# Variance of two tiles on quarters of the array, key transposes in halves, and the last key tile among the value products

## The chip, the cores and the metric

The kernel runs on one core of one Trainium2 chip. The engines of a core each work through a queue of their own, in order: PE (TensorE, the matrix products; its weight loads are listed apart as PEld), DVE (VectorE), ACT (ScalarE), POOL (GpSimd) and SP (SyncE, which issues the transfers). The metric is the time of one execution in microseconds, lower is better, median of three runs.

## The reference

A decoder trunk of two layers on 16 learned and 256 given tokens, T = 272 in all, D = 2048: an RWKV-7 mixer, a squared-ReLU MLP, a gated linear attention (GLA), another MLP. The change touches the RWKV-7 mixer alone:

```python
r = xr @ w_rkv[0]; k = xk @ w_rkv[1]; v = xv @ w_rkv[2]
w_log = -softplus(-(w0 + tanh(xw @ w1) @ w2)) - 0.5
a = sigmoid(a0 + (xa @ a1) @ a2)
g = sigmoid(xg @ g1) @ g2
kk = k * k_k per head; kk = kk / max(sqrt(sum(kk * kk)), 1e-12)
k = k * (1 + (a - 1) * k_a);  decay = exp(-exp(w_log))
# per token and head: S <- S diag(decay) + (S (-kk)) (kk a)^T + v k^T;  y = S r
mu = mean(y); var = mean(square(y - mu))            # per head of 64
y = (y - mu) * rsqrt(var + eps) * ln_w + ln_b
bonus = sum(r * k * r_k) * v
out = ((y + bonus) * g) @ w_o
```

There are 32 heads of 64, so a tile of 128 rows holds two heads, and the 2048 features are 16 such tiles.

## The kernel before

Everything is kept transposed, features on the 128 partitions and tokens along the free axis. A weight comes as `raw` tiles of 128x1024 float32. ACT rounds one to `hi` (L140), DVE subtracts to get `lo` (L141), and PE makes three products for each 128x128 piece (`mm3`, L163 to L165): `hi` by the high part of the activations, `hi` by their low part, `lo` by the high part. So every weight tile needs ACT, then DVE, then 24 products of PE. There are three buffers for `raw` and two each for `hi` and `lo`.

The RWKV mixer has these stages, one after the other. The receptance products come first, with the low-rank (LoRA) products for decay and learning rate between them (`lora`, sigmoids at L478 and L479, kept in `hres` for the first eight tiles and in `ca` for the others). Then the **key stage**, a loop over the 16 tiles `f` of keys. `keyproj` makes the products of tile `f` from two weights. `front` scales them (`kk`, L619) and squares them (`sq`, L620). `rest(f - 1)` stands between the two weights of the next tile and does all that follows for a tile: `sums` (L604, four quarter products of 64x64 for the squared norm of `kk` in bank `pm` and for the bonus of the tile before in bank `pu`), three exponentials, a logarithm (L633 to L638), some fifteen small operations on DVE (L300 is the helper of all element-wise ones, L641 makes `kn` for the bonus), and transfers of the results to memory (`ard`, `bkd`). From tile 9 on `scores` also makes the masked score matrices (`AM`, products L537), and from tile 12 on `inv`, the inversion of a triangular system, runs as 30 steps of two DVE operations (`upd`, `sysA`).

After the last tile come the **value products** `v_proj`, also sixteen tiles with two weights each. They are cut into units of one `mm3` each, and `R(n)` runs n units; the code puts the work of the recurrence between them. For a group g of eight heads' pairs and a chunk c of 64 tokens this is: `centre` (values transposed and centred into bank `pm`, copied out by ACT at L745), `keys` (keys transposed by L752 into a `pt` bank and a `pm` bank, copied out at L754), `inner`, `state`, `solve`, `learn`, `emit`. `merge`, `scores` and `inv` are in between again. `norm(g)` is a generator, run tile by tile for the four tiles of g: per tile the square, one full-array float32 product with a block matrix of ones (the variance, L841, bank `pry`), two products with the gate weights `g2` (L844), a logarithm and an exponential on ACT, and three operations on DVE. `split(g)` then makes the output products' operands of `hres`.

The order on PE is written out by hand (`manual_schedule`) in these parts, while the end of one such block and the start of the next may interleave. On ACT, DVE and SP a scheduler decides at build time by program order, by estimated times and by priority: the weight loads have a priority of 2000, small transfers of 4000, all else none. The before calls the first value products like this:

```python
        for i in ((0, 128), (128, 320)):
            fetch(1, ARs, ard, i)
        ahead()
        with tc.manual_schedule(engines={mybir.EngineType.PE}):
            R(43)
```

`fetch(1, ARs, ...)` loads the block of `AR` for the next score matrices from memory, into a pool (`win`) that takes the place of the key stage's pool `early`.

## Time and profile before

| | |
|---|---|
| median of three runs | 2384.78 us (2384.59 to 2385.85) |
| the profiled execution | 2384.69 us, span 2382.6 us |
| mean granted clock of PE | 0.998 |
| receptance and low-rank products end, key stage begins | about 160 us |
| value products begin | about 267 us |
| output products of the RWKV mixer begin to stand alone | about 546 us |
| DVE busy over the span | 1608.1 us |
| ACT busy over the span | 1251.8 us |

The span is the profiled execution from its first to its last instruction; times in a timeline count from its start. In the list of waits a row names an engine, the line that waited, what released it, and then the total, the count and the longest wait. In a timeline a row has start, duration, engine, line, operation, output and inputs with their shape, and how many instructions of a kind were joined into the row (`x4`); brackets hold the idle time before it and what ended it. A float32 product leaves two records. In a table by stretches each engine's busy time stands with the number of its instructions, then the granted clock of PE as a share of full speed, the share of the transfer engines and their rate.

### The profile page before, as it was taken

To read this page: it belongs to the slowest core of one execution; us is meant where nothing else is said; L and a number is where in the kernel's file an instruction comes from. 1 tells how busy PE (TensorE), PEld (TensorE's weight loads), DVE (VectorE), ACT (ScalarE), POOL (GpSimd) and SP (SyncE) were. 2 spreads that over 40 slices of the span, in tenths; PEclk is the share of its full clock that TensorE was granted. 3 is DMA by queue.
4 is the path that set the end of the run, shared out by engine and by line. 5 is a ranking of instruction groups with operands and counts; after the bars stand their busy time and mean duration, and the time that the engine had idled before them with its cause. 6 is when DMAs were issued, how large, how long until landed. Compare 5 with 4: busy or idle time off the path is not lost. (4 is left out here: it accounts for less than half of the span.)

```text
span 2382.6 us, 48158 instructions
## 1 busy us (share of the span) xinstructions
PE 2349.0 (99%) x19753; PEld 2231.2 (94%) x19753; DVE 1608.1 (67%) x2702; ACT 1251.8 (53%) x1995; POOL 12.4 (1%) x37
## 2 busy tenths in 40 slices
PE   9999899999999999999999999999999999999998
PEld 8888898889999999999999999999999999999997
DVE  8868976848555555555556777767666666666666
ACT  6478554556555344345344556645555445445444
POOL 0000000000000000000000000000000000000000
PEclk9999999999999999999999999999999999999999
DMA  5468654535555555555555555445555555555554
GB/s 209 160 205 301 225 172 142 150 93 173 186 189 192 188 192 188 190 191 188 193 187 192 193 172 176 163 172 197 180 201 203 201 199 202 203 199 200 203 201 170
DMA packets 157003, 449.18 MB, mean 189 GB/s; under 512 B 33968, under 2 KB 49968, under 8 KB 156784
## 3 DMA queue, kind: packets, MB, share of 16 engines
q1 hardware_dynamic: 156784, 446.11, 54.7%
q8 instruction: 155, 2.54, 0.4%
q14 instruction: 64, 0.52, 0.1%
HBM read 429.93 MB, written 14.42 MB: 186 GB/s over the span
## 5 line engine op out<-in xcount | busy, mean ns | idle before, releaser
L141 DVE TENSOR_TENSOR lo<-raw,hi 128x1024 fp32r<-128x1024 f32 (+1 forms) x818 | 927.0, 1140 | 529.9 <-ACT hi L140 521.5
L140 ACT CAST hi<-raw 128x1024 fp32r<-128x1024 f32 (+1 forms) x818 | 794.2, 978 | 926.9 <-PE pj L164 535.8
L163 PE MATMUL pj<-x,hi 128*128 128x272 f32 (+1 forms) x2624 | 747.6, 285 | 4.3 <-DVE r L300 1.8
L165 PE MATMUL pj<-x,lo 128*128 128x272 f32 (+1 forms) x2624 | 732.3, 279 | 2.2 <-DVE lo L141 2.2
L164 PE MATMUL pj<-x,hi 128*128 128x272 f32 (+1 forms) x2624 | 732.8, 279 | 0.2 <-DVE x L240 0.2
L163 PEld LDWEIGHTS pj<-x,hi 128*128 128x128 f32 x2624 | 497.6, 190 | 17.1 <-issue 8.4
L165 PEld LDWEIGHTS pj<-x,lo 128*128 128x128 f32 x2624 | 497.8, 190 | 3.7 <-DVE lo L141 3.4
L164 PEld LDWEIGHTS pj<-x,hi 128*128 128x128 f32 x2624 | 497.9, 190 | 3.4 <-issue 1.8
L196 PE MATMUL pj<-x,hi 128*128 128x512 f32 x1280 | 419.8, 382 | 0.1
L197 PE MATMUL pj<-x,lo 128*128 128x256 f32 x1280 | 348.7, 273 | 0.0
L196 PE MATMUL pj<-h,hi 128*128 128x512 f32 x1008 | 330.3, 382 | 0.0
L163 PE MATMUL pj<-h,hi 128*128 128x272 f32 (+1 forms) x1040 | 290.1, 279 | 0.0
L164 PE MATMUL pj<-h,hi 128*128 128x272 f32 (+1 forms) x1040 | 290.1, 279 | 0.0
L165 PE MATMUL pj<-h,lo 128*128 128x272 f32 (+1 forms) x1040 | 290.1, 279 | 0.0
L197 PE MATMUL pj<-h,lo 128*128 128x256 f32 x1008 | 274.8, 273 | 0.0
L196 PEld LDWEIGHTS pj<-x,hi 128*128 128x128 f32 x1280 | 241.9, 189 | 34.1 <-DVE x L1063 0.4
L197 PEld LDWEIGHTS pj<-x,lo 128*128 128x128 f32 x1280 | 245.8, 192 | 0.1
L196 PEld LDWEIGHTS pj<-h,hi 128*128 128x128 f32 x1008 | 190.5, 189 | 26.5
L163 PEld LDWEIGHTS pj<-h,hi 128*128 128x128 f32 x1040 | 196.6, 189 | 0.0
L164 PEld LDWEIGHTS pj<-h,hi 128*128 128x128 f32 x1040 | 196.6, 189 | 0.0
L165 PEld LDWEIGHTS pj<-h,lo 128*128 128x128 f32 x1040 | 196.6, 189 | 0.0
L197 PEld LDWEIGHTS pj<-h,lo 128*128 128x128 f32 x1008 | 193.5, 192 | 0.0
(276 smaller groups left out, 2071.3 us busy)
## 6 DMA issues: line engine op xcount, KB each, us to landing
raw<-mlp_w_d SPq DMA_DIRECT2D x512, 512.0 KB, 3.3
raw<-gla_in_d SPq DMA_DIRECT2D x98, 512.0 KB, 3.2
raw<-w_rkv_d SPq DMA_DIRECT2D x80, 512.0 KB, 3.9
raw<-gla_o_d SPq DMA_DIRECT2D x32, 512.0 KB, 3.2
raw<-w_r_d SPq DMA_DIRECT2D x16, 512.0 KB, 3.2
raw<-rw_oQ_d SPq DMA_DIRECT2D x16, 512.0 KB, 3.5
raw<-lora_d SPq DMA_DIRECT2D x8, 512.0 KB, 3.4
raw<-rw_oA_d SPq DMA_DIRECT2D x8, 512.0 KB, 3.4
```

The costliest lines, as they stand in the source:

```text
L140: nc.scalar.copy(hi[:, h], raw[:, h])
L141: nc.vector.tensor_tensor(out=lo[:, h], in0=raw[:, h], in1=hi[:, h].bitcast(F32), op=ALU.subtract)
L163: nc.tensor.matmul(out, hi[:, ws], xh, start=first, stop=False)
L164: nc.tensor.matmul(out, hi[:, ws], xl, start=False, stop=False)
L165: nc.tensor.matmul(out, lo[:, ws], xh, start=False, stop=last)
L196: nc.tensor.matmul(wide, hi[:, ws], xt, start=kt == 0, stop=False)
L197: nc.tensor.matmul(one, lo[:, ws], xt[:, 0], start=False, stop=kt == nk - 1)
```

## The change

Four edits, all in `rwkv`.

1. `norm(g)` makes the four squares of its group first (four buffers), and takes two tiles together: each variance is two products with quarters of the array, four in a row, the first tile's in bank `pry`, the second's in bank `pm` with its halves exchanged. The second tile's logarithm is then two activations of half the partitions.
2. The gate weights `g2` are fetched two tiles ahead.
3. `keys` transposes 64-row halves, sixteen products in place of eight, by turns into the `pt` and the `pm` bank, both of which it takes at the start.
4. The key stage's loop ends at tile 15; `rest(15)` runs after the fourth value unit, `sums(None)` (the last tile's bonus sums) after the sixteenth, and the pool `win` and the fetches of `AR` follow behind. `rest` runs at a priority of 600.

```diff
@@ -651,15 +651,14 @@
             nc.gpsimd.tensor_copy(WC[:, f], W[:, C : 4 * C1 : C1])
 
         with tc.manual_schedule(engines={ENG.PE}):
-            for f in range(KT + 1):
-                if f < KT:
-                    ps = (self.pry if f % 3 == 2 else self.pj)()[:, :T]
-                    keyproj(f, ps, 0)
+            for f in range(KT):
+                ps = (self.pry if f % 3 == 2 else self.pj)()[:, :T]
+                keyproj(f, ps, 0)
                 if f:
-                    rest(f - 1)
-                if f < KT:
-                    keyproj(f, ps, 1)
-                    front(f, ps)
+                    with tc.high_priority(offset=600):
+                        rest(f - 1)
+                keyproj(f, ps, 1)
+                front(f, ps)
                 if f == 1:
                     xv = [self.t(self.xp, [P, 2, T], "x", KT, F32R) for _ in range(KT)]
                     for kt in range(KT):
@@ -683,15 +682,7 @@
                 if f > 12:
                     for _ in range(6):
                         next(inv, None)
-            sums(None)
-        early.close()
-
-        win = ExitStack()
-        kp = win.enter_context(tc.tile_pool(name="win", bufs=1, side="right", reuse_waits="tile"))
-        ARs.append(self.t(kp, [P, 8, 320], "AR1"))
-        AMs.append(self.t(kp, [P, 2, 16, 128], "AM1"))
-        AMrs.append(self.t(kp, [64, 16, 64], "AMr"))
-        sb = self.t(kp, [P, 8, HEAD], "S")
+
         bank = lambda x: x.rearrange("p (h v) -> p h v", h=8)
         uvs, ras, bkts, rys, pSs = {}, {}, {}, {}, {}
 
@@ -731,6 +722,8 @@
             yield
 
 
+        heads = lambda x: x.rearrange("p (h v) -> p h v", h=8)
+
         def centre(g, c):
             full, n, nr = geom(c)[:3]
             pv = self.pm()
@@ -745,13 +738,14 @@
                 nc.scalar.copy(x[:nr, 8 * e : 8 * e + 8], pv[64 * e : 64 * e + nr].rearrange("p (h v) -> p h v", h=8))
 
         def keys(g, c):
-            bkts[g, c] = self.t(kp, [P, 8, P], "bkt", 1)
-            for e in range(2):
-                pb = self.pm() if e else self.ptr()
-                for p in range(4):
-                    nc.tensor.transpose(pb[:, p * P : (p + 1) * P], BKs[c > 1][:, 4 * e + p, c % 2 * 128 : c % 2 * 128 + 128],
-                                        self.ident)
-                nc.scalar.copy(bkts[g, c][:, 4 * e : 4 * e + 4], pb.rearrange("p (h v) -> p h v", h=4))
+            x = bkts[g, c] = self.t(kp, [P, 8, P], "bkt", 1)
+            pbs = [self.ptr(), self.pm()]
+            for f in range(8):
+                for q in range(2):
+                    nc.tensor.transpose(pbs[q][:, f * HEAD : (f + 1) * HEAD],
+                                        BKs[c > 1][half(q), f, c % 2 * 128 : c % 2 * 128 + 128], self.ident[half(q), half(q)])
+            for q in range(2):
+                nc.scalar.copy(x[:, :, half(q)], heads(pbs[q]))
 
 
         def inner(g, c):
@@ -825,27 +819,44 @@
             nc.scalar.copy(hres[:, 8 * g : 8 * g + 8, c * C : c * C + nr], ry[:, :, :nr])
 
         def norm(g):
+            fs = range(4 * g, 4 * g + 4)
+            sqs, g2s = {}, {}
 
             def square(f):
-                sq = self.t(kp, [P, T], "ysq", 2)
-                nc.scalar.activation(sq, hres[:, f], AF.Square)
-                return sq
-
-            nxt = square(4 * g)
+                if f in fs:
+                    sqs[f] = self.t(kp, [P, T], "ysq", 4)
+                    nc.scalar.activation(sqs[f], hres[:, f], AF.Square)
+
+            def load(f):
+                if f in fs:
+                    g2s[f] = self.t(kp, [P, 2, P], "g2", 2)
+                    nc.sync.dma_start(g2s[f], ap["g2"][f])
+
+            def spread(sq, va, x, y):
+                nc.scalar.activation(sq[x], va[y], AF.Ln, scale=1.0 / HEAD, bias=self.eps[GN_EPS][x])
+
+            for i in range(2):
+                load(fs[i])
+            for i in range(4):
+                square(fs[i])
             yield
-            for f in range(4 * g, 4 * g + 4):
-                sq = nxt
-                g2 = self.t(kp, [P, 2, P], "g2", 2)
-                nc.sync.dma_start(g2, ap["g2"][f])
-                va = self.pry()[:, :T]
-                nc.tensor.matmul(va, self.bones, sq, start=True, stop=True)
+            for f in fs:
+                if f % 2 == 0:
+                    vas = [self.pry()[:, :T], self.pm()[:, :T]]
+                    for i in range(2):
+                        for q in range(2):
+                            nc.tensor.matmul(vas[i][half(q ^ i)], self.bones[half(q), half(q)], sqs[f + i][half(q)],
+                                             start=True, stop=True)
                 pg = (self.ptr() if g else self.pu())[:, :T]
                 for i in range(2):
-                    nc.tensor.matmul(pg, g2[:, i], gs[i], start=i == 0, stop=i == 1)
-                nc.scalar.activation(sq, va, AF.Ln, scale=1.0 / HEAD, bias=self.eps[GN_EPS])
+                    nc.tensor.matmul(pg, g2s[f][:, i], gs[i], start=i == 0, stop=i == 1)
+                load(f + 2)
+                if f % 2 == 0:
+                    spread(sqs[f], vas[0], slice(0, P), slice(0, P))
+                    for q in range(2):
+                        spread(sqs[f + 1], vas[1], half(q), half(1 - q))
+                sq = sqs[f]
                 nc.scalar.activation(sq, sq, AF.Exp, scale=-0.5)
-                if f < 4 * g + 3:
-                    nxt = square(f + 1)
                 nc.vector.scalar_tensor_tensor(out=sq, in0=hres[:, f], scalar=self.vec("ln_w", f), in1=sq, op0=ALU.mult,
                                                op1=ALU.mult)
                 tt(rr[f], rr[f], sq, ALU.add)
@@ -959,11 +970,25 @@
         nothing = iter(())
         units1 = ((2, 0), (2, 1), (3, 0), (3, 1), (4, 0))
         self.split_parts = 2
+        ahead()
+        with tc.manual_schedule(engines={ENG.PE}):
+            R(4)
+            with tc.high_priority(offset=600):
+                rest(KT - 1)
+            R(12)
+            sums(None)
+        early.close()
+
+        win = ExitStack()
+        kp = win.enter_context(tc.tile_pool(name="win", bufs=1, side="right", reuse_waits="tile"))
+        ARs.append(self.t(kp, [P, 8, 320], "AR1"))
+        AMs.append(self.t(kp, [P, 2, 16, 128], "AM1"))
+        AMrs.append(self.t(kp, [64, 16, 64], "AMr"))
+        sb = self.t(kp, [P, 8, HEAD], "S")
         for i in ((0, 128), (128, 320)):
             fetch(1, ARs, ard, i)
-        ahead()
-        with tc.manual_schedule(engines={mybir.EngineType.PE}):
-            R(43)
+        with tc.manual_schedule(engines={ENG.PE}):
+            until(43)
             for c, e in units1:
                 some(inv, 5)
                 R(13)
```

`half(q)` is rows 64q to 64q + 63, `ENG` is `mybir.EngineType`, `until(43)` runs what is left of the first 43 units.

How this moves instructions is shown at three places. The first is ACT at the end of the low-rank products and the beginning of the key stage, from the last sigmoids (L478, L479) to the first `kk` and `sq` of the key stage; `iW` at L636 is an exponential of `rest`. Before:

```order
L478 ACTIVATE iW_1782<-pm_1778,vecs_126 128x272
L479 ACTIVATE ca_1777<-pry_1779,vecs_126 128x272
L496 ACT_TABLE_LOAD
L140 CAST hi_1870<-raw_1868 128x1024
L636 ACTIVATE iW_1898<-hres_72 128x272
L636 ACTIVATE iW_2047<-hres_72 128x272
L140 CAST hi_1926<-raw_1924 128x1024
L619 ACTIVATE kk_1863<-pj_1802,vecs_126 128x272
L620 ACTIVATE sq_1864<-kk_1863 128x272
```

The two exponentials stand behind both sigmoids and the one table load. In the change, the same stretch of ACT:

```order
L478 ACTIVATE iW_1782<-pm_1778,vecs_126 128x272
L636 ACT_TABLE_LOAD
L636 ACTIVATE iW_1898<-hres_72 128x272
L140 CAST hi_1870<-raw_1868 128x1024
L636 ACTIVATE iW_2047<-hres_72 128x272
L479 ACT_TABLE_LOAD
L479 ACTIVATE ca_1777<-pry_1779,vecs_126 128x272
L140 CAST hi_1926<-raw_1924 128x1024
L496 ACT_TABLE_LOAD
L619 ACTIVATE kk_1863<-pj_1802,vecs_126 128x272
L620 ACTIVATE sq_1864<-kk_1863 128x272
```

They stand ahead of the last sigmoid, and three table loads are there in place of one. Some 65 rows earlier the exponentials `W` (L633) of the first two tiles move ahead of sigmoids in the same way, with four table loads before and now; on PE the small products `pm`, `pry` of those sigmoids come later.

The second place is DVE in the value products, where tile 15's operations stand (`kn` from bank `pj`, then `bk`, `ar`, and the `kn` of L641 that the last sums take). Before, around the `lo` of the fifth value weight (`lo_3659`):

```order
L300 TENSOR_TENSOR kn_3474<-pj_3360,kn_3474 128x272
L300 TENSOR_TENSOR upd_3503<-sysA_2014 64x234
L300 TENSOR_TENSOR bk_1789<-kn_3474,iW_3473 128x4x64
L141 TENSOR_TENSOR lo_3659<-raw_3656,hi_3658 128x512 x2
L300 TENSOR_TENSOR bk_1789<-kn_3474,iW_3473 128x16
L300 TENSOR_TENSOR ar_1791<-r_30_104,W_1797 128x4x64
L300 TENSOR_TENSOR ar_1791<-r_30_104,W_1797 128x16
L641 SCALAR_TENSOR_TENSOR kn_3474<-r_30_104,vecs_126,kn_3474 128x272
```

In the change, behind the `lo` of the second value weight (`lo_3497`):

```order
L141 TENSOR_TENSOR lo_3497<-raw_3494,hi_3496 128x512 x2
L300 TENSOR_TENSOR bk_1788<-kk_3338,iW_3391 128x16
L300 TENSOR_TENSOR kn_3506<-pj_3360,kn_3506 128x272
L300 TENSOR_TENSOR upd_3348<-sysA_2014 64x184
L300 TENSOR_TENSOR bk_1789<-kn_3506,iW_3505 128x4x64
L300 TENSOR_TENSOR bk_1789<-kn_3506,iW_3505 128x16
L300 TENSOR_TENSOR ar_1791<-r_30_104,W_1797 128x4x64
L300 TENSOR_TENSOR ar_1791<-r_30_104,W_1797 128x16
L641 SCALAR_TENSOR_TENSOR kn_3506<-r_30_104,vecs_126,kn_3506 128x272
```

The tile's operations now stand ahead of the later steps of the inversion (`upd` of 64x184 in place of 64x234), so ten steps more come behind them. Ahead of the `lo` of the eleventh value weight DVE has 547 instructions before and 545 in the change. On SP the two fetches of `AR` stand behind three value weights' loads fewer.

The third place is PE at `norm(1)`, where the values of the second group have just been centred (`pm`, L739 before, L732 in the change). Before:

```order
L739 MATMUL pm_5969<-cst_125,hres_72 64x128 x8
L841 MATMUL pry_5983<-ysq_5873,cst_125 128x272
L844 MATMUL pt_5985<-gs_2_76,g_903_5981 128x272
L844 MATMUL pt_5985<-gs_3_77,g_903_5981 128x272
L163 MATMUL pj_6007<-x_5995,hi_5946 128x272
```

In the change:

```order
L732 MATMUL pm_6020<-cst_125,hres_72 64x128 x8
L848 MATMUL pry_6032<-ysq_5918,cst_125 64x272 x2
L848 MATMUL pm_6033<-ysq_5920,cst_125 64x272 x2
L852 MATMUL pt_6038<-gs_2_76,g_893_5914 128x272
L852 MATMUL pt_6038<-gs_3_77,g_893_5914 128x272
L163 MATMUL pj_6062<-x_6050,hi_5997 128x272
```

The variance of the group's second tile has moved up to the first one's place, into the bank that `centre` has just filled.

## The prediction

> **What bounds the kernel now.** I read the head of the page first.
>
> ```profile
> span 2382.6 us, 48158 instructions
> PE 2349.0 (99%) x19753; PEld 2231.2 (94%) x19753; DVE 1608.1 (67%) x2702; ACT 1251.8 (53%) x1995; POOL 12.4 (1%) x37
> ```
>
> TensorE (PE) has work for all but 33.6 us of the span, so time can only be had where PE stands still or where its work itself shrinks. Everything that the change touches lies in the RWKV stage. Next I read the waits of PE (total, times, longest), of which these lie in that stage:
>
> ```profile
> PE pu L604 <- DVE kn L641: 2.5, 1, 2.5
> PE pm L604 <- ACT sq L620: 1.9, 3, 0.9
> PE pj L163 <- DVE r L300: 1.8, 1, 1.8
> PE pt L537 <- DMA AR<-ard: 1.7, 1, 1.7
> PE pj L163 <- ACT hres L884: 1.4, 1, 1.4
> ```
>
> The timeline puts the three single waits for `kn`, AR and `hres` into the first value products, within 25 us:
>
> ```profile
> 274.71 0.38 PE L163 MATMUL pj<-x,hi 128*128 128x272 f32 x1 [1.40 <-ACT hres L884]
> 283.04 0.68 PE L604 MATMUL pu<-kn,cst 64*64 64x272 f32 x4 [2.50 <-DVE kn L641]
> 295.64 0.83 PE L537 MATMUL pt<-AR,BK 64*128 64x128 f32 x10 [1.72 <-DMA AR<-ard]
> ```
>
> The last query is the work of VectorE (DVE) by stretches (start and end, length, DVE busy and its count, PE's granted clock):
>
> ```profile
> 160.00:264.00 104.00, 91.64 (x219) 1.00 0.83 277
> 264.90:305.10 40.20, 37.96 (x102) 0.96 0.65 208
> 306.00:393.00 87.00, 52.95 (x117) 1.00 0.53 157
> 393.60:434.50 40.90, 39.12 (x103) 1.00 0.48 141
> 442.60:481.80 39.20, 37.11 (x101) 1.00 0.40 121
> 482.00:546.00 64.00, 32.36 (x65) 1.00 0.34 109
> ```
>
> This decides most of what follows. In the second, fourth and fifth stretch, in each of which a triangular inversion of 60 small operations runs, DVE is busy for 94 to 96% of the time: there PE follows DVE, and what PE saves comes back as a longer wait. From 306 to 393 and after 482 DVE has room, and a saving on PE shows in the end.
>
> **The last key tile among the value products.** A unit is three products with one 128-row piece of a weight. Before, the last sums (the wait of 2.5 us) stand behind 32 value units, in the change behind 16, and the tile's DVE work comes earlier to match. Its wait has a second price, the granted clock right behind it (here in the eleventh column of the windows of all engines):
>
> ```profile
> 284.60:287.80 3.20, 3.20 (x17) 3.20 (x16) 3.00 (x10) 0.33 (x1) 0.00 (x0) 0.50 0.44 124
> ```
>
> PE runs there at half clock for 3.2 us, which costs 1.6. Were PE alone to decide, the change would take out 1.4 + 2.5 + 1.7 (the transfer of AR, issued three weights earlier in SP's queue) + 1.6 = 7.2 us. That is the upper end. The lower one comes from DVE, and from PE behind it:
>
> ```profile
> 288.98 0.69 DVE L141 TENSOR_TENSOR lo<-raw,hi 128x512 fp32r<-128x512 f32 x1 [1.37 <-ACT hi L140]
> 305.10 0.68 DVE L141 TENSOR_TENSOR lo<-raw,hi 128x512 fp32r<-128x512 f32 x1
> 306.46 0.28 PE L163 MATMUL pj<-x,hi 128*128 128x272 f32 x1
> ```
>
> The row at 305.10 is the `lo` half of the eleventh value weight, which PE begins at about 306.4. DVE has 547 instructions ahead of that row before and 545 in the change, so nearly the same work must be done first, and what can be won is DVE's idle time, 40.20 - 37.96 = 2.2 us (1.37 of it at 288.98, where it waited for ACT). The row moves to 302.9 and ends at 303.6; PE, whose two `hi` products (0.23) come ahead of the first `lo` product, begins at 303.3, or 3.1 us earlier. The two instructions fewer, at 91.64 / 219 = 0.42 us each, make it 3.9. The old waits then turn into several short ones in front of `lo` products. A wait of 2 us among them may halve the clock once more, which would take 1.6 off. I take **+4.0** (range 1.5 to 7.2), by the DVE rows, since they count work and the upper end counts on PE alone.
>
> By the Trainium skill ("TensorE: Matmul & The Clock Gate", Part 1: The HAM clock gate) the clock falls after one idle window of about 3.4 us. Here it fell behind a wait of 2.50 us, so the trace does not bear the length out; by the page, shorter waits would leave the clock alone and the 1.6 would be safe.
>
> **The priority that comes with it.** `rest` now runs at a higher priority, and the scheduler moves exponentials on ACT across sigmoids: one table load (1.28 us) stood right before the key stage's first sums, now there are three.
>
> ```profile
> 158.56 0.49 ACT L479 ACTIVATE ca<-pry,vecs 128x272 f32<-128x272 f32 x1
> 159.07 1.28 ACT L496 ACT_TABLE_LOAD   x1
> 160.37 1.04 ACT L140 CAST hi<-raw 128x1024 fp32r<-128x1024 f32 x1
> 162.97 1.04 ACT L140 CAST hi<-raw 128x1024 fp32r<-128x1024 f32 x1 [0.90 <-PE pj L164]
> 164.43 0.43 ACT L620 ACTIVATE sq<-kk 128x272 f32<-128x272 f32 x1
> 165.75 0.68 PE L604 MATMUL pm<-sq,cst 64*64 64x272 f32 x4
> ```
>
> Two more loads are 2 x 1.28 = 2.56 us in this queue. Its idle time of 0.90 takes some; `sq` was ready at 164.86 and PE came for it at about 165.7, which hides another 0.8. The first sums come 2.56 - 0.90 - 0.80 = 0.9 us later, and behind them on PE the second half of the tile's key products, with nothing to cover it: **-0.9** (0 to -1.7). Around 115 us an exponential moves ahead of two sigmoids, so ACT's part of the low-rank products comes later and PE's small products with it. No row prices that; it is between 0 and a load with a following activation, 1.28 + 0.43 = 1.7. I take **-0.3**, near the low end because the number of loads there stays the same.
>
> In key tiles 9 to 12 the second mask now stands behind `kn` on DVE, so the sums find `kn` sooner; the waits for `sq`, 1.9 us in all, keep their cause. **+0.3** (0 to 0.6).
>
> **Key transposes in halves.** The full ones, and for the new form the transposes of 64 rows in the GLA stage:
>
> ```profile
> 332.50 0.60 PE L752 MATMUL pt<-cst,BK 128*128 128x128 f32 x4
> 333.03 0.66 PE L752 MATMUL pm<-cst,BK 128*128 128x128 f32 x4
> 333.44 0.36 PE L163 MATMUL pj<-x,hi 128*128 128x272 f32 x1
> 1349.50 0.28 PE L165 MATMUL pj<-x,lo 128*128 128x272 f32 x1
> 1349.71 0.41 PE L1200 MATMUL pt<-cst,vs 64*128 64x64 f32 x6
> 1350.05 0.38 PE L163 MATMUL pj<-x,hi 128*128 128x272 f32 x1
> ```
>
> Eight full transposes take 0.94 us, or about 0.85 when the second bank is free. The six half ones are three pairs, one on each half of the rows; from the first start to the next product they take 0.34, and as a pair overlaps in itself and goes over from the full array (1349.71 - 1349.50 - 0.12 = 0.09) only once, I put a pair at (0.34 - 0.09) / 3 = 0.08. Eight pairs are 0.66, with the way over 0.75: 0.1 less between full-array products. Beside tiled products the full form pays the way over and back, and the half form does not: 0.3 less. A gain of 0 to 0.4 a call holds both. The first call needs both banks at once, and `pm` comes free only at 333.03, so it loses 0.2. Of the eight calls, three lie in 306 to 393 (-0.2 + 0.3 + 0.1 = **+0.2**), one beside tiled products after 482 (**+0.3**), and four where PE follows DVE.
>
> **Variance on quarters.** The full product, and four quarters as they stand in the key stage:
>
> ```profile
> 405.19 0.62 PE L841 MATMUL pry<-ysq,cst 128*128 128x272 f32 x2
> 405.65 0.85 PE L844 MATMUL pu<-gs,g 128*128 128x272 f32 x3
> 172.12 0.45 PE L604 MATMUL pm<-sq,cst 64*64 64x272 f32 x2
> 172.74 0.38 PE L163 MATMUL pry<-x,hi 128*128 128x272 f32 x1
> ```
>
> Two tiles cost 2 x 0.46 = 0.92; four quarters 0.62, with the 0.09 for going over 0.71: 0.21 less a pair. `norm(2)` and `norm(3)`, four pairs, lie after 482: **+0.8**. The other four pairs and four key calls are at most 0.8 + 1.2 = 2.0 us of saving in the stretches that DVE holds. There `norm(1)` also gets a new wait: its second tile needs `pm`, which the centred values fill just before, and which ACT must first copy out:
>
> ```profile
> 443.20 1.17 ACT L745 COPY uv<-pm 64x512 f32<-64x512 f32 x2 [0.67 <-PE pm L739]
> ```
>
> Behind that product wait the gate products, two units and the key transposes, 1.2 us at most. PE waits 1.8 us for DVE at the end of the same stretch (for `r`, in the list above), which covers it. Together **+0.4** (-1.2 to +2.0). The half-height Ln adds one activation a pair on ACT, which is far from full there. The earlier load of the gate weights removes no wait, for PE has none on `g2`: 0.
>
> **The sum.** 4.0 - 0.9 - 0.3 + 0.3 + 0.2 + 0.3 + 0.8 + 0.4 = +4.8 us. The profiled execution took 2384.69 us, 2.1 more than its span and 0.1 less than the median of the runs; 2384.69 - 4.8 = **2379.9 us**. A difference under 0.2% (4.8 us: from 2380.0 to 2389.6) counts as no change, so the forecast stands on that edge.
>
> **Rivals.** *PE gets all of it*: DVE's waiting steps give way to the `lo` rows where it counts, and the value products give 7.2, not 4.0: 2379.9 - 3.2 = 2376.7. For it: after 306 DVE has 34 us of room to do the steps later; against it: the 94% above. Chance 0.27. *The wait only changes its name*: PE runs into DVE at once, waits 2 us or more for one `lo`, and the clock halves again, so the value term is between 0 and 1.5: 2382.4 to 2383.9. For it: the clock fell behind a wait of 2.5. Chance 0.14. *A table switch drains ACT* for as long as an activation lasts, 0.49, twice: 2380.9. Against it: `ca` ended at 159.05 and the cast began at 160.37, 1.32 us later with the load in between. Chance 0.03. The Trainium skill has such a drain ("ScalarE: Activation LUTs", What ACT_TABLE_LOAD costs): a switch is about 2.7 us there with it, and 1.28 of these agree with the row; by the page the two would cost some 2.8 us more. *Slower*: `rest` at high priority pushes the next weight's `lo` back in the fifteen key tiles, whose stretch has DVE at 88%. One operation of 0.42 us a tile is 6.3 us: 2386.2. It decides from 4.8 / 15 = 0.32 a tile on, and makes 2389.6 at 0.65. Against it: in tiles 9 to 12 the `lo` rows keep their place on DVE. Chance 0.10. The forecast keeps 0.46.
>
> **Range and chances.** By the bounds of its terms the forecast's own range is 2377.0 to 2382.5, and a little over half of it, 0.26 of the 0.46, lies under 2380.0. Faster by over 0.2%: 0.27 + 0.26 = 0.53 and 0.01 of the drain. Slower by over 0.2%: the tail of the last rival and what I did not think of, 0.07. Within: 0.39. The range takes in the first two rivals but for their tails: **2374.0 to 2385.0**.
>
> **What would show it.** Right: the waits of 2.5 on `kn` and 1.7 on AR are gone, PE waits in short pieces for `lo` from 265 to 305, the eleventh value weight begins 3 to 5 us sooner after the key stage, two more table loads stand by the first key sums with 1 us of PE idle, a pair of variances takes 0.6 to 0.7. Wrong: a granted clock of 0.5 again there; more wait for `lo` in the key stage; a wait for `pm` in `norm(1)` that isn't paid back by 482; savings that stay whole in the stretches I gave to DVE.

## The result and the profile after

The changed kernel took 2381.69 us (median of 22 runs, 2380.17 to 2384.38), the kernel before 2385.33 (22 runs, 2384.29 to 2389.10). The ratio is 0.9984, with a 95% interval of 0.9978 to 0.9989: faster, by 3.6 us in the medians, and a little less than the 0.2% that was called a difference. The forecast was 4.8 us faster, on the edge of that bound; it gave faster by more than 0.2% a chance of 0.53 and a smaller change 0.39, and the smaller change came.

The head of the page after, and the rows of PE's waits that answer to those of before:

```profile
span 2379.0 us, 48378 instructions
PE 2346.9 (99%) x19849; PEld 2224.7 (94%) x19849; DVE 1607.7 (68%) x2702; ACT 1260.6 (53%) x2005; POOL 12.1 (1%) x37
```

```profile
PE pj L165 <- DVE lo L141: 4.3, 7, 1.8
PE pm L604 <- ACT sq L620: 3.0, 4, 0.9
PE pj L163 <- DVE r L300: 0.9, 1, 0.9
PE pm L848 <- ACT uv L738: 0.7, 1, 0.7
```

The waits for `kn` (2.5), AR (1.7) and the copy of `hres` (1.4) are gone. In their place PE waits longer for `lo`, once 1.8 us; for `sq` it waits once more; and a wait for `pm` is new. Sums of waits don't give the time, though. What does is the start of the same PE instruction in both traces, place by place:

| place on PE (its time before) | before to after | lead of the change | gained since the row above |
|---|---|---|---|
| end of the first sums of squares (12) | 12.04 to 11.14 | 0.90 | 0.90 |
| first low-rank products (111) | 111.00 to 110.12 | 0.88 | -0.02 |
| a late low-rank group (149) | 148.96 to 148.87 | 0.09 | -0.79 |
| first key sums | 165.75 to 166.65 | -0.90 | -0.99 |
| sums of tile 15 | 268.73 to 269.31 | -0.58 | 0.32 |
| third score products of the values | 307.25 to 304.06 | 3.19 | 3.77 |
| last chunk of the first group | 400.07 to 396.73 | 3.34 | 0.15 |
| centring of the second group | 442.03 to 439.29 | 2.74 | -0.60 |
| second group's third chunk | 493.88 to 491.38 | 2.50 | -0.24 |
| its fourth chunk | 505.07 to 502.29 | 2.78 | 0.28 |
| end of the RWKV mixer | 599.25 to 595.85 | 3.40 | 0.62 |
| last product | 2372.26 to 2368.70 | 3.56 | 0.16 |

The first row belongs to no edit: the instructions there are the same in both kernels. In the fourteen traces of this study, of kernels that all begin alike, that place lies between 10.87 and 13.13 us. So about 0.9 us of the 3.56 in this pair of profiles is chance, and the change is worth some 2.7 us in the traces; the medians' 3.6 has an interval of 2.6 to 5.2, which takes in both. The last row belongs to no edit either: from the end of the mixer to the last product the kernels with an edit lie between 1.45 us behind the kernel before and 1.01 ahead. A difference of a few tenths in a single trace is therefore a reading, not a proof.

The rows behind the two largest terms, first PE and DVE in the value products:

```profile
269.31 0.45 PE L604 MATMUL pm<-sq,cst 64*64 64x272 f32 x2 [0.57 <-ACT sq L620]
281.53 0.38 PE L165 MATMUL pj<-x,lo 128*128 128x272 f32 x1 [0.57 <-DVE lo L141]
302.67 1.28 DVE L141 TENSOR_TENSOR lo<-raw,hi 128x512 fp32r<-128x512 f32 x2
303.40 0.38 PE L165 MATMUL pj<-x,lo 128*128 128x272 f32 x1 [1.78 <-DVE lo L141]
```

The row at 302.67 is the `lo` of the eleventh value weight, which started at 305.10 before; PE stands for 1.78 us in front of it. The granted clock stays whole and DVE is nearly full, in the windows over all engines and over DVE alone:

```profile
264.00:306.00 42.00, 39.07 (x345) 36.07 (x338) 40.98 (x111) 19.94 (x42) 0.00 (x0) 1.00 0.70 225
264.90:305.10 40.20, 39.21 (x106) 1.00 0.70 224
```

Then ACT and PE at the first key sums, where three table loads now stand:

```profile
158.61 1.28 ACT L636 ACT_TABLE_LOAD   x1
161.62 1.28 ACT L479 ACT_TABLE_LOAD   x1
164.35 1.28 ACT L496 ACT_TABLE_LOAD   x1
166.17 0.43 ACT L620 ACTIVATE sq<-kk 128x272 f32<-128x272 f32 x1
166.65 0.68 PE L604 MATMUL pm<-sq,cst 64*64 64x272 f32 x4 [0.91 <-ACT sq L620]
```

`sq` comes at 166.60 in place of 164.86, and PE waits 0.91 us for it.

### The profile page after: what moved, and what is told of

Read it like the earlier page. It is cut to its first block, busy times and chain, and to the rows that moved or that the text cites. A ratio compares the mean times of both kernels' runs of the same rounds, so it can differ in the third digit from the quotient of the medians.

```text
span 2379.0 us, 48378 instructions
## 1 busy us (share of the span) xinstructions
PE 2346.9 (99%) x19849; PEld 2224.7 (94%) x19849; DVE 1607.7 (68%) x2702; ACT 1260.6 (53%) x2005; POOL 12.1 (1%) x37
## 3 DMA queue, kind: packets, MB, share of 16 engines
q8 instruction: 156, 2.56, 0.4%
```

## The experiments

Times are medians, each beside runs of the kernel before on the same chip. Leads are the starts of the same PE instructions against the profile of before, as in the table above; a gain of a stretch is the difference of two leads, so delays ahead of it drop out (what another engine got done during them does not). "Value stretch" is from the sums of tile 15 to the third score products, 38.52 us before and 34.75 in the change, a gain of 3.77.

### The priority from tile 3 on

```diff
-                if f:
+                if f > 3:
                     with tc.high_priority(offset=600):
                         rest(f - 1)
+                elif f:
+                    rest(f - 1)
```

> The changed kernel, but the key tiles 0 to 2 run their rest without the higher priority, so that ACT has the order of before around the sigmoids and at the first key sums (seven table loads there, not nine). Theory (the two added loads and the delayed sigmoids cost 0.8 + 1.0 us in the change, and nothing else of the priority matters in those tiles): the wait at the first key sums goes, the key stage begins about 0.8 us sooner against the first products and its first sums 1.0 us sooner still; 1.8 us under the change, ratio to before 0.9976 (0.9970 to 0.9982). Rival (the key stage is held by its weights' transfers, so an earlier first sum is lost again): the lead at the first sums is 1.8 us, but at the last key sums under 0.6, and the time is within 0.5 us of the change.

This version, called late priority below, took 2380.71 us against 2385.83, ratio 0.9979 (0.9970 to 0.9989). ACT's order ahead of the key stage is that of before again, with one table load, and PE finds `sq` ready:

```profile
158.17 1.28 ACT L496 ACT_TABLE_LOAD   x1
164.86 0.68 PE L604 MATMUL pm<-sq,cst 64*64 64x272 f32 x4
```

The lead over before is 0.89 us at the first low-rank products and 0.90 at the first key sums (164.86 in place of 165.75, start-up included), where the change goes from 0.88 to -0.90. So the two places are worth 1.8 us, as expected, and at the sums of tile 15 the lead is 1.78, not lost again. The value stretch gains 3.53, the rest goes as in the change. In time the difference to the change is 1.0 us in the medians, with intervals 2.6 and 4.5 us wide, so the traces show it and the times do not.

### Each edit alone

The move alone (with the priority) is the changed kernel with `keys` and `norm` of before; the other two are the kernel before with the new `norm` or the new `keys`, word for word as in the diff of the change.

> The kernel before with the last key tile among the value products and the priority, variance and transposes as before. Theory: it has all of the gain of the value products (3.8 us) and all of the loss at the sigmoids and the first sums (-1.8), and +0.3 in the key stage: 2.3 us under before, ratio 0.9990 (0.9984 to 0.9996). Rival (the transposes and the variance pay for the gain): within 0.8 us of before.

> The kernel before with the variance on quarters (and the earlier gate weights) alone. Theory: 0.6 us from the four pairs after 482 us, nothing from the four pairs in the stretches that DVE paces, where the wait for pm in norm(1) shows on PE (0.7 us and more) and is paid back by 482: 0.6 us under before, ratio 0.9997 (0.9992 to 1.0002). Rival (the pm wait costs in the end): 0.3 to 0.8 us over before.

> The kernel before with the key transposes in halves alone. Theory: +0.4 us from the three calls in 306 to 393 together (the first one loses, since both banks are taken at once), nothing from the four in the stretches that DVE paces, +0.3 from the last: 0.7 us under before, ratio 0.9997 (0.9992 to 1.0002). Rival (all eight calls count): 0.3 each, 2 us or more under before.

| version | median (before 2385.83) | ratio, 95% interval | value stretch | 307 to 400 | 400 to 442 | 442 to 494 | 494 to 599 |
|---|---|---|---|---|---|---|---|
| move alone | 2383.79 | 0.9992 (0.9982 to 1.0001) | 3.76 | -0.61 | -0.60 | -0.02 | -0.02 |
| variance alone | 2385.06 | 0.9997 (0.9987 to 1.0006) | -1.38 | -0.03 | -0.60 | -0.91 | 0.63 |
| transposes alone | 2384.99 | 0.9997 (0.9988 to 1.0007) | 0.16 | 0.49 | -0.29 | 0.11 | 0.25 |
| the change | 2381.69 | 0.9984 (0.9978 to 0.9989) | 3.77 | 0.15 | -0.60 | -0.24 | 0.90 |

The move has the whole gain of the value stretch; the six traces that have both move and priority, and the inversion on DVE, gain 3.48 to 3.77 there. The transposes bring 0.5 between 307 and 400 and 0.25 in the last call, and little in the stretches between; by calls the first loses 0.24 and the second to fourth gain 0.27, 0.19 and 0.27. That the move alone loses 0.61 between 307 and 400 is left unexplained; with that loss it is only 0.8 us ahead at the end of the mixer, start-up taken out, where its theory had 2.3. The variance brings 0.6 where `norm(2)` and `norm(3)` run and loses 0.91 between 442 and 494, where `norm(1)` runs and where its theory had the wait for `pm` paid back by 482: there the rival was right. All three ratios came out where the theory had them, but none of the three intervals leaves out 1 or the rival's figure, so the times decide nothing between them. The -0.6 from 400 to 442 is no edit's: the move alone has it with the old `norm` and `keys`, and so has the kernel before without its first inversion, further down (-0.59). All the other traces but that of the products on POOL have -0.3 to -0.6 there too, so it lies most likely in the one profile of before.

The -1.38 of the variance alone in the value stretch is most likely chance too, and instructive: its order there is that of before, and its waits read

```profile
282.78 0.45 PE L604 MATMUL pu<-kn,cst 64*64 64x272 f32 x2 [2.49 <-DVE kn L641]
295.13 0.49 PE L537 MATMUL pt<-AR,BK 64*128 64x128 f32 x4 [3.14 <-DMA AR<-ard]
```

The clock did not halve behind the first wait here (why is shown in the last section), so PE came to the AR products at 291.99, 1.9 us sooner than before. The transfer was issued 1.7 us sooner (289.00 against 290.73) but took 6.0 us in place of 4.8 and landed only 0.5 us sooner. So PE waited 1.4 us longer, and the clock halved behind this wait instead. The change issues that transfer at 278.68, has it at 283.71 and needs it at 290.16, so it also takes a source of spread away.

### Without the first inversion's work on DVE

```diff
             for s in range(1, 31):
...
-                tt(w, ...)
-                tt(X[:n, :m, s + 1 :], X[:n, :m, s + 1 :], w, ALU.add)
+                if b:
+                    tt(w, ...)
+                    tt(X[:n, :m, s + 1 :], X[:n, :m, s + 1 :], w, ALU.add)
                 yield
```

> The kernel before without the 60 DVE operations of the first inversion (the first group's triangular matrices are left as they are, so its results are not the reference's). Theory (in the value products PE follows DVE, and the stalls of before are work that stands in DVE's queue): without these 25 us of DVE work the waits for hres (1.4) and kn (2.5) and the half clock behind them go although nothing was moved; only the wait for the transfer of AR may stay. From the last key sums but one to the third score products behind it some 5.5 us less than before. Rival (the stalls come from where the last sums stand): the wait for kn stays over 2 us.

> The changed kernel without the same 60 operations (the first group's results are not the reference's). Theory: the waits for lo between 265 and 305 (0.6 and 1.8 in the change) go, and the stretch is 2 to 3.5 us shorter than in the change; against the kernel before without the inversion it gains 2 us or less, the wait for AR, where the change gained 3.8. Rival (DVE does not pace the stretch in the change): within 0.5 us of the change there.

One run each: 2384.62 and 2381.35 us, beside 2386.16 before. The value stretch gains 2.37 and 5.19, not 5.5 and 5.8 to 7.3. The second is 1.42 more than the change gains and 2.82 more than the kernel before without the inversion, where 2 to 3.5 and at most 2 were expected. So both expectations were missed, because a wait for `kn` of nearly 2 us stands in both, though DVE has idle time everywhere. The timeline of DVE in the kernel before without the inversion:

```profile
276.01 0.43 DVE L300 TENSOR_TENSOR r<-r,hres 128x272 f32<-128x272 f32 x1
278.76 0.51 DVE L300 TENSOR_TENSOR bk<-kn,iW 128x256 f32<-128x256 f32 x2 [2.32 <-DMA bkd<-bk]
280.81 0.49 DVE L642 SCALAR_TENSOR_TENSOR kn<-r,vecs,kn 128x272 f32<-128x272 f32 x1
```

and its waits of PE:

```profile
PE pu L605 <- DVE kn L642: 1.8, 1, 1.8
PE pt L537 <- DMA AR<-ard: 1.7, 1, 1.7
```

The instruction ahead of `kn` writes a buffer `bk` whose old content is still being transferred to memory; it waits 2.32 us for that. So DVE's queue is not the only thing that makes `kn` late; with the queue gone, the transfer of `bk` holds it for nearly as long. In the change the same instruction runs without a wait. The wait for `hres` (1.4) did go without the inversion.

The second kernel differs from the change by more than the work that is left out, for the schedule came out otherwise. Behind the sums of tile 15 the change has 36 value products on PE, 4.98 us, before the last sums; without the inversion 61 are recorded there, 9.91 us with the wait. On DVE the tile's last `kn` stands behind two more value weights' `lo` (four rows), and the `bk` ahead of it waits 1.59 us for its transfer. So PE gets a wait that the change does not have:

```profile
281.34 0.45 PE L605 MATMUL pu<-kn,cst 64*64 64x272 f32 x2 [1.96 <-DVE kn L642]
```

Nor does the gain hold over a longer stretch. From the first key sums to the sums of tile 15 the two kernels lose 1.06 and 1.78, where the change gains 0.32; from the first key sums to the third score products the change gains 4.09 and the same kernel without the inversion 3.41. What the inversion's work on DVE costs is therefore not shown by these two runs. What they do show in the second kernel is that PE's waits for `lo` between 265 and 305 are gone, as expected.

### The move without the priority

```diff
-                    with tc.high_priority(offset=600):
-                        rest(f - 1)
+                    rest(f - 1)
...
-            with tc.high_priority(offset=600):
-                rest(KT - 1)
+            rest(KT - 1)
```

> The changed kernel with the last tile moved, but no higher priority for any tile. DVE has the same instructions ahead of the eleventh value weight's lo give or take two, but the last sums' kn stands behind the third value weight's lo in place of ahead of it. Theory (DVE paces the value products): PE waits 1.5 us or more for kn in front of the last sums, the waits for lo behind it shrink by about as much, and from the last key sums but one to the third score products behind it takes what it takes in the change, within 0.6 us. Rival (each wait adds to the time): the stretch is longer by the kn wait. Ahead of the key stage and at its first sums the 1.8 us are back, as with late priority.

2379.77 us in one run beside 2385.39, with 1.2 us of luck at the start. Ahead of the key stage and at the first key sums nothing is lost against before, as expected. The value stretch gains 1.27, 2.50 less than in the change, so the first theory falls and its rival holds: the waits added up. The rows of PE, and the windows of all engines behind the first:

```profile
274.32 0.45 PE L604 MATMUL pu<-kn,cst 64*64 64x272 f32 x2 [2.04 <-DVE kn L641]
303.82 0.38 PE L165 MATMUL pj<-x,lo 128*128 128x272 f32 x1 [1.91 <-DVE lo L141]
```

```profile
276.00:277.00 1.00, 1.00 (x6) 1.00 (x6) 1.00 (x3) 0.00 (x0) 0.00 (x0) 0.50 0.14 53
277.00:278.00 1.00, 1.00 (x7) 1.00 (x6) 1.00 (x5) 0.00 (x0) 0.00 (x0) 0.50 0.59 94
```

PE waits 2.04 us for `kn`, the expected new stall, and runs at half clock behind it from 275.3 to 278.7, 3.4 us. That costs about 1.7 (half of 3.4) of the 2.5; the other 0.8 is the wait itself as far as DVE does not take it back. Without the clock the theory would have been off by 0.8 where it allowed 0.6. Whether the clock falls hangs on where the wait lies in time (last section), and this is one trace. Over the whole mixer, from the first sums of squares to its end, this kernel gains 2.45 us and the change 2.50, for it does not lose the 1.8 us ahead of the key stage.

### The priority without the move

The kernel before, with `rest(f - 1)` under the priority and nothing else.

> The kernel before with the higher priority for all tiles, the last tile left in its place. Theory (move and priority are needed together): the last sums still stand behind more than 32 units and their kn behind the fifth value weight's lo, so PE waits 1 us or more for kn, and the transfer of AR, now behind two more weights, is waited for 1.7 us or more; from the last key sums but one to the third score products behind it no more than 1 us is gained, and the 1.8 us ahead of the key stage and at its first sums are lost. Rival (the priority alone does it): the kn wait goes and the stretch gains 2.5 us or more.

PE's two waits, and the windows of all engines around the second:

```profile
284.86 0.35 PE L163 MATMUL pj<-x,hi 128*128 128x272 f32 x1 [2.14 <-DVE kn L300]
301.14 0.59 PE L537 MATMUL pt<-AR,BK 64*128 64x128 f32 x2 [5.02 <-DMA AR<-ard]
```

```profile
300.00:306.00 6.00, 4.86 (x28) 4.67 (x29) 5.60 (x16) 0.00 (x0) 0.00 (x0) 0.50 0.98 301
```

2395.20 us in one run beside 2385.39. The value stretch loses 6.02: PE waits 2.14 us for the first `kn` operation of tile 15, ahead of the last sums and not at them (there 0.19), and 5.02 for AR, whose fetch is issued 5.1 us later than before (295.85 against 290.73), and both are followed by half clock, for 3.4 and 6.8 us. The theory was right that the priority alone gains nothing and loses the 1.8 us in front (0.79 and 0.99). So in that stretch the gain is neither the move's nor the priority's: in these single traces the priority alone loses 6 us, and the move alone gains a third of what both gain together, or, with the 1.7 us of half clock taken off, about four fifths.

### Another bank for the variance in norm(1)

```diff
-                    vas = [self.pry()[:, :T], self.pm()[:, :T]]
+                    vas = [self.pry()[:, :T], (self.pu() if g == 1 else self.pm())[:, :T]]
```

> The changed kernel, in norm(1) with the second tile's variance in a pu bank in place of pm. Theory (PE follows DVE up to 478 us, so PE's wait for the copy out of pm is paid back): the waits for pm at 442 and at the transposes go (1.2 us sooner at the next products), the wait for r at 478 grows by about as much, and from 485 on the times are those of the change within 0.3 us. Rival: 0.7 us or more is kept to the end of the stage.

2383.28 us in one run beside 2386.16. The wait for `pm` goes and another takes its place, PE's rows being

```profile
444.90 0.50 PE L852 MATMUL pt<-gs,g 128*128 128x272 f32 x1 [2.03 <-ACT bkt L748]
479.50 0.38 PE L163 MATMUL pj<-x,hi 128*128 128x272 f32 x1 [1.73 <-DVE r L300]
```

The second tile's gate products need a `pt` bank, which ACT frees by copying the keys out, and ACT now does that behind a weight's cast and both logarithms. Behind that wait the clock halves, which it does not in the change (windows of all engines):

```profile
445.64:449.06 3.42, 3.42 (x34) 2.98 (x35) 2.47 (x9) 0.83 (x2) 0.00 (x0) 0.50 0.63 196
```

The wait for `r` grew from 0.94 to 1.73 as expected, but from 442 to 494 the lead falls by 2.53, in the change by 0.24. Of these 2.29 us the half clock accounts for about 1.7. DVE lost time as well: its operations of `norm` moved ahead of the inversion's steps in its order, and it stood in front of them, idle for 2.4 us between 442 and 453 where the change has 0.6. The theory failed: a wait of PE that the clock follows was not paid back. But DVE's order moved with the bank, which neither theory had, and what the bank alone would do is not shown.

### Three versions meant to be better

Quarters in `norm(2)` and `norm(3)` alone; quarters everywhere but in `norm(1)`, and the first key call with full transposes; and, in each step of the first and third inversion, the product `upd` on POOL. All three have the priority from tile 3 on.

```diff
-                tt(w, X[:n, s : s + 1, s + 1 :]..., X[:n, :m, s : s + 1]...)
+                (nc.gpsimd if b in (0, 2) else nc.vector).tensor_tensor(out=w, in0=X[:n, s : s + 1, s + 1 :]...,
+                    in1=X[:n, :m, s : s + 1]..., op=ALU.mult)
```

> The version with priority from tile 3 on, with the variance on quarters in norm(2) and norm(3) alone, one tile at a time with a full product in norm(0) and norm(1). Theory (in the traces of the change and of the variance alone, quarters cost 0.6 us in norm(0) and 0.2 to 0.9 in norm(1) and bring 0.6 after 494): about 0.9 us under the version with late priority, ratio to before 0.9974 (0.9967 to 0.9981). Rival (what the quarters cost in norm(0) and norm(1) is taken back where PE follows DVE): the same as late priority, 0.9979.

> The version with late priority, with norm(1) alone tile by tile as before (its pm wait goes) and the first key call in full transposes as before (its wait for both banks goes). Theory: 0.3 to 0.5 us from norm(1), 0.2 from the key call, 0.6 in all under late priority, ratio 0.9976 (0.9968 to 0.9984); between the first inner products and the third solve of the second group the lead grows by 0.5 against late priority. Rival (DVE paces there whatever PE does): no change in the lead at that solve.

> The version with late priority, with the first of the two operations of each step of the first and third inversion (30 x 0.4 us each) on POOL, which does nothing there. Theory (DVE paces the value products and 394 to 423): the waits for lo and AM there shrink, 1 to 2.5 us less than late priority, if POOL's steps keep up with the inversion's due time. Rival 1 (POOL's operations take several times DVE's, or hold DVE up at the shared memory port): the inversion ends late and PE waits for it in merge, up to tens of us more. Rival 2 (DVE does not pace): within 0.5 us of late priority.

| version | median | before | ratio, 95% interval | 442 to 494 |
|---|---|---|---|---|
| priority from tile 3 | 2380.71 | 2385.83 | 0.9979 (0.9970 to 0.9989) | -0.24 |
| and quarters in norm(2), norm(3) | 2380.38 | 2386.16 | 0.9979 (0.9970 to 0.9988) | 0.31 |
| and quarters but in norm(1), full first key call | 2380.87 | 2385.39 | 0.9978 (0.9969 to 0.9987) | 0.10 |
| and `upd` on POOL | 2394.18 | 2385.39 | 1.0036 (1.0023 to 1.0050) | 1.52 |

With the old form in `norm(1)` the stretch from 442 gains 0.3 to 0.55 against late priority, as expected, and the second version's first key call takes 1.06 us again, as before. The 0.6 us that the first version was to gain from the old form in `norm(0)`, between 400 and 442, did not come: that stretch has -0.62 there, -0.32 in late priority. In time they cannot be told from late priority; the first came out at 0.9979, the figure of its rival. All three of them beat the kernel before; that they beat the change is likely by the traces and not shown by the times.

POOL made it slower. Its group of instructions, and PE's two largest waits:

```profile
L569 POOL TENSOR_TENSOR upd<-sysA 64x30 f32<-64x30 f32 (+14 forms) x60 | 43.2, 720 | 33.1 <-DVE sysA L300 33.1
```

```profile
PE pj L165 <- DVE lo L141: 11.8, 13, 2.4
PE pt L537 <- DVE AM L300: 7.8, 3, 5.8
```

One product takes 720 ns there, against 319 for the same product on DVE in late priority, and each step hands over twice, while DVE, which works in order, stands in front of the step with the next `lo` behind it. The value stretch is 4.5 us longer than before, 8.0 longer than with late priority, and from 400 to 442 another 8.1 are lost, 5.8 of them in one wait for the masks, which half clock follows until 425.5. Rival 1 was right in the time, 13.5 us over late priority, and in POOL being slower; DVE's own steps were not held up by it (323 ns in place of 319 for `sysA`), and PE waited for `lo` and the masks, not in `merge`.

## Why the prediction was right

**The value products** were put at +4.0 and measured +3.77. The working through DVE's rows holds: the eleventh weight's `lo` was to start 2.2 + 0.8 = 3.0 us sooner, and counted from the sums of tile 15 it starts 3.01 sooner (36.37 us behind them before, 33.36 in the change). PE stands for 1.78 us in front of the products that take this `lo`, while DVE is busy for 39.21 of 40.20 us: there DVE does hold PE. The granted clock of 0.50 behind the old stall is gone, and the new longest wait of 1.78 did not bring it back. Its theory, that DVE paces the stretch whatever PE does, was too strong. The move without the priority shows that a wait of PE for `kn` is paid for (2.5 us longer, of which 1.7 is clock), and the kernel before without the inversion shows that the old stall had a second cause in waiting, the transfer of the buffer `bk`. Neither upsets the number, which was made from DVE's rows and their order in the change. That less work on DVE would shorten the stretch further was not shown, for the change without the inversion came out in another order.

**The priority.** At the first key sums -0.9 was forecast and -0.99 measured, and late priority shows that the two table loads are the cause. At the sigmoids the forecast had -0.3 and the trace -0.79: that term was mis-sized. It was left near zero because the number of loads did not rise. Late priority, where the exponentials stand behind the sigmoids again, has no loss there (0.01), so their order is the cause; that the low-rank products wait for the sigmoids' banks and pass the delay on is the likely way, and not shown.

**The key stage** was put at +0.3. The trace has +0.32, yet among the versions with priority from tile 3 on, whose key stage is the same, that stretch gains 0.88 in one and loses 0.65 in another. It can't be told.

**Transposes**: -0.2, +0.3, +0.1 forecast for the first three, -0.24, +0.27, +0.19 measured in the transposes alone, and +0.28 for the last one in the change (+0.3). The fourth, counted to a stretch that DVE holds, lies ahead of it and gained 0.27. The price of 0.08 us a pair was a little high. One call beside tiled products has eight pairs 0.06 apart, in the trace of the change:

```profile
444.80 0.22 PE L745 MATMUL pm<-cst,BK 64*128 64x64 f32 x1
444.86 0.22 PE L745 MATMUL pm<-cst,BK 64*128 64x64 f32 x1
444.93 0.23 PE L745 MATMUL pm<-cst,BK 64*128 64x64 f32 x1
```

**Variance**: +0.8 in `norm(2)` and `norm(3)` came out as 0.62. In `norm(2)` the period from pair to pair went from 5.53 (before, 521.86 to 527.39) to 5.43 us (variance alone, 524.62 to 530.05), so a pair saves 0.10 and not 0.21: the way back to the full array costs another 0.1 (0.32 us from the last quarter's start to the gate product's, 0.23 from a full product's), which the sum left out. Four pairs at 0.10 make 0.4 of the 0.62; where the other 0.2 come from is open.

**The stretches that DVE holds** were put at +0.4 (-1.2 to +2.0) and came to about -0.8 from 400 to 494, of which 0.6 is most likely the profile of before. The wait for `pm` in `norm(1)` was there (0.69, and 0.49 at the transposes and the gate products behind it), 1.4 us of lead were lost at 449, and 1.16 came back by 494, as the wait for `r` fell from 1.79 to 0.94. That is the hiding that was forecast, short by 0.24.

**The whole.** The number came nearer than its terms did. Without the start-up the trace's terms add up to 2.7 us where 4.8 were forecast: the stretches that DVE holds are 1.2 short, the sigmoids 0.5, the value products and the variance 0.2 each. The error lies in the small terms; the large one held.

Of the rivals, *PE gets all of it* did not occur, nor did the clock halve again in the change, but it did in the move without the priority, behind a wait of the length that the rival named, though for `kn` and not for `lo`. *A table switch drains ACT*: `sq` came 1.74 us later where 2.56 less ACT's idle time of 0.90 makes 1.66, which leaves no room for two drains of 0.49; in the trace of the change each of the three loads also begins within 0.02 us of the end of the instruction ahead of it, and the next one starts within 0.02 us of its end. *Slower by lo rows pushed back* is refuted: PE has no wait for `lo` in the key stage, before or after.

## What to carry to other kernels

When two engines run close behind one another, make the sum from the rows of the engine that paces, up to the instruction that is waited for, and not from the waits that go: 7.2 us of them were there, half clock included, and 3.8 came out. Test a move and a priority apart, and over the whole stage: in the value stretch the priority on top of the move brought 2.5 us, but up to the end of the mixer the two kernels gain the same, 2.45 and 2.50. A priority reaches further than the place it is meant for: here it cost 1.8 us in front of the stage, by exponentials that moved across sigmoids, and leaving it off for three tiles gave them back. Where a scheduler orders the instructions, look at the orders before reading an experiment: leaving out work can move other work.

## What was not expected of the hardware

PE's clock fell to half for 3.4 us behind single waits of 2.50 (before), 2.04 (the move without the priority), 2.03 (another bank), 3.14 (the variance alone) and, in the kernel before without the inversion, 1.5 us behind one of 1.81; it did not behind 2.49 (the variance alone, at 282.78), 1.96 (the change without the inversion), nor behind 1.78, 1.77 and 1.91 for `lo`. So the length of a wait does not decide it.

The traces point to what does. In all fourteen the granted clock changes only at whole multiples of 3.413 us from the moment that it first rose: in the profile before it was whole for 82 such steps, half for one and whole for 612. Of the steps between 14 and 2360 us, all ten that began at full clock and had PE idle for 1.94 us or more were followed by half clock, and of those with 1.80 or less none was. Between 1.81 and 1.88 both occur: of four such steps one was, that of the wait of 1.81 for `kn`. At a program's start one step with 1.51 us of idle time was followed by half clock too (quarters everywhere but in `norm(1)`). A wait of 2.5 us that a boundary cuts can so leave the clock alone, and one of 1.8 within a step can halve it. The step with the wait of 2.50 and the one behind it, in the profile before (windows of all engines):

```profile
281.10:284.51 3.41, 1.47 (x11) 1.06 (x12) 3.41 (x10) 1.24 (x3) 0.00 (x0) 1.00 0.41 133
284.51:287.93 3.42, 3.42 (x17) 3.42 (x17) 3.09 (x11) 0.41 (x2) 0.00 (x0) 0.50 0.47 135
```

The same for the variance alone, where a boundary cuts the wait of 2.49 into 1.88 and 0.61, and then for its wait of 3.14:

```profile
278.75:282.17 3.42, 1.53 (x14) 1.33 (x12) 3.36 (x10) 1.14 (x2) 0.00 (x0) 1.00 0.34 131
282.17:285.58 3.41, 2.80 (x23) 2.39 (x24) 3.41 (x11) 1.15 (x3) 0.00 (x0) 1.00 0.45 154
292.41:295.82 3.41, 0.69 (x12) 0.72 (x14) 2.94 (x9) 0.64 (x2) 0.00 (x0) 1.00 1.07 337
295.82:299.23 3.41, 3.41 (x21) 3.19 (x19) 2.47 (x8) 0.00 (x0) 0.00 (x0) 0.50 0.93 299
```

The Trainium skill ("TensorE: Matmul & The Clock Gate", Part 1: The HAM clock gate) has a window of about 3.4 us that runs free of the program, and the traces agree with its length, 3.413 us; but where the page has the clock fall after an idle window, here 1.94 us of idle time within one was enough.

And the start of a program varies as much as the edits that are studied here: the same instructions reached the same place between 10.87 and 13.13 us in fourteen traces. The latest of these is the one with half clock at the start, from 8.83 to 12.24; the others lie between 10.87 and 12.07.
